# A recurrent layer's first operands ahead of its norm's root, and block-sum steps two and four in the twelve-tile down pairs

## The chip, the cores and the metric

The kernel runs on one core of a Trainium2 chip. The core has TensorE (matrix products, into PSUM), VectorE, ScalarE, GpSimd and SyncE, called PE, DVE, ACT, POOL and SP in the profile; PEld is TensorE's loading of the stationary operand. Each engine works through its own instructions in order and waits for others by semaphores. Weights come from device memory by DMA; the SP and POOL queues issue these transfers. The metric is device time of one execution in microseconds (us); lower is better.

## The reference, cut to what matters

The model is an encoder trunk of two residual layers over 256 tokens of 2048 features, in float32. Layer 0 mixes tokens by attention, layer 1 by a recurrent block; behind each mixer stands a gated feed-forward network of width 5632.

```python
for i in range(DEPTH):                       # DEPTH = 2
    h = rms_norm(x, norm_mix[i])             # x * rsqrt(mean(x*x) + EPS) * gain
    mix = attention_mixer(h, ...) if i % 2 == 0 else recurrent_mixer(h, ...)
    x = x + mix
    x = x + swiglu(rms_norm(x, norm_ffn[i]), ffn_w_gate[i], ffn_w_up[i], ffn_w_down[i])

def recurrent_mixer(h, w_in, conv_w, conv_b, w_a, b_a, w_i, b_i, lam, w_out):
    xb, yb = jnp.split(h @ w_in, 2, axis=-1)
    yb = gelu(yb)
    xb = depthwise_conv_centred(xb, conv_w, conv_b)      # width 4
    h_fwd, h_bwd = rg_lru(xb, ...), rg_lru(xb, ..., reverse=True)   # gates: block-diagonal products of xb
    return ((h_fwd + h_bwd) * yb) @ w_out

def swiglu(h, w_gate, w_up, w_down):
    return (silu(h @ w_gate) * (h @ w_up)) @ w_down
```

## The kernel before

**Products in three matmuls.** Every float32 operand is split into a rounded high part and the remainder as low part, and a product is three matmuls: high by high, high by low, low by high. Weights arrive in halves of 512 KB (eight 128x128 tiles). `load_half` loads one by the SP queue into `raw`, ScalarE rounds it to `hi` (L141) and VectorE subtracts to get `lo` (L142). Five buffers of each kind rotate, so these two engines can prepare halves ahead of TensorE.

**Pairs and block-sum steps.** In the feed-forward network `project_pair` works on two 512-wide columns of weights at once. A step `n` covers two 128-row tiles of the inner dimension. An ordinary step loads two halves, one for each column, and makes eight products (two columns, two token halves, two tiles), each 128x512. For steps listed in `forms` it makes seven products instead, by sums and differences of the blocks, as in fast matrix multiplication: `seven_forms` builds the weight sums, `x_forms` the operand sums. The weight sums start from one half loaded by SP, a second 256 KB load (`wx`), and a block `sr` that the POOL queue has fetched two such steps ahead, in two buffers, as a 512 KB copy and a 256 KB transfer that adds to it. ScalarE and VectorE then work at L319 to L328. Four of the seven products go to four extra PSUM banks (`p1, q5, q6, q7`, the tag `pm`) and `merge` (L401 to L405) adds these up once per pair, behind the last block-sum step; three go to the ordinary accumulators.

**The feed-forward network in parts.** The hidden width of 44 tiles is worked in `PARTS` of 12, 16 and 16 tiles. A part is three or four units (gate and up columns; each gives four hidden tiles) and then two down pairs, which multiply the part's hidden tiles back to 2048 columns and add to the residual `x_tok` (L581, L589). Units use block-sum steps `THREE = (1, 3, 5)`, the second, fourth and sixth step; so do down pairs of sixteen tiles. Down pairs of twelve tiles have six ordinary steps. `pair_plan` lets the first steps of a pair serve both columns and the last ones each column alone, so that the first column can be finished while the second goes on.

A unit's result is turned and split for the next product by work put into `owed` (a transpose at L860, sixteen copies at L866, the split at L873 and L874, and `x_forms` where a later step wants them). `settle` emits a few entries of it at a time, between steps of what follows.

**Who sets the order.** TensorE's order is that of the program text. On the other engines a planner places instructions by their readiness in its own timeline. `in_line` and `follow` pin some: casts and low parts keep their order among themselves, and `not_after(i, ahead)` makes the low part of the half `ahead` places on follow instruction `i`, which `settled` carries out.

**The norm of the recurrent layer.** `Norm.add(c)` is called as each of the four 512-wide columns of the residual is complete: sums of squares on ScalarE (L491), transposes on VectorE (L496), copies on both (L503), then four operand tiles with their gains (L478, L479). The root of the mean square is left out of the operands; it is multiplied in later. `finish` takes it (L520 to L530): a reduction, a logarithm and an exponential on ScalarE, one correction on VectorE, and a diagonal `ndg`. `stage`, emitted `NORM = 20` TensorE steps later, spreads the root over all partitions by matmuls with ones (L536) and ScalarE copies it to `nrb` (L538). For the last column, `first` calls `finish` right behind the squares, and the copies of that column must follow the root's last ScalarE instruction and the diagonal:

```python
fields["behind"] = self.finish() if last else [line.get(e) for e in ("act", "dve")]
...
behind = fields["behind"] if last else [line.get(e) for e in ("act", "dve")]
```

The first TensorE work of the recurrent layer is `project_two`: two columns of the input projection, 32 steps of three 128x256 matmuls (L409 to L411). The first 24 read only operand tiles of the first three columns; the last eight read the four tiles of the last column. It is a generator: `conv_branch` (the multiplication by the root, L905, and the convolution) for the first column is emitted before the last four steps of the second. The gates of the first block follow 24 steps into the next projections (`WHEN_FIRST`).

Of the kernel before, what the change touches and what calls it, by code (L numbers as in the profile page):

```python
# [12 lines left out]
F32 = mybir.dt.float32  # L13
F32R = mybir.dt.float32r
AF = mybir.ActivationFunctionType
ALU = mybir.AluOpType
AX = mybir.AxisListType

P = 128
# [9 lines left out]
THREE, TWO, SHORT = (1, 3, 5), (2, 5), 6  # L29
# [5 lines left out]
FOUR = WIDE // P  # L35
# [4 lines left out]
GRID_W = 64  # L40

WARM = 10
NORM = 20
FIRST = 6
KEY_SCALE = 20
KEY_TURN = (62, 68)
# [24 lines left out]
def trunk(ctx, tc, w, out):  # L71
    nc = tc.nc
    act, dve, pool, pe, sync = nc.scalar, nc.vector, nc.gpsimd, nc.tensor, nc.sync
# [13 lines left out]
    def nm(s):  # L87
        uid[0] += 1
        return f"{s}_{uid[0]}"
# [6 lines left out]
    newest = {}  # L96

    def follow(i, j):
        tc.add_manual_dep(
            i.ins, j.ins.name,  # L100
            mybir.DependencyInfo(mybir.DependencyClass.NoSync, mybir.DependencyReason.DATA),
            reason="order",
        )
        return i


    line = {}

    def in_line(eng, i):
        if eng in line:  # L110
            if line[eng] is not None:
                follow(i, line[eng])
            line[eng] = i
        return i

    due = {}

    def not_after(i, ahead=3):
        due.setdefault(taken[0] + ahead, []).append(i)

    def settled(i, n):
        for k in [k for k in due if k <= n]:
            for j in due.pop(k):
                follow(i, j)

    def load_half(src, n, pieces=1, then=None, before=None):
        raw = wp.tile([P, HALF, P], F32, tag="raw", name=nm("raw"), bufs=5)
        hi = wp.tile([P, HALF, P], F32R, tag="hi", name=nm("hi"), bufs=5)
        lo = wp.tile([P, HALF, P], F32R, tag="lo", name=nm("lo"), bufs=5)
        for i in range(pieces):  # L130
            sl = slice(i * n // pieces, (i + 1) * n // pieces)
            newest["load"] = sync.dma_start(out=raw[:, sl, :], in_=src[:, sl, :])
        newest["raw"] = raw
        if then:
            then()
        if before:
            before(raw)
        for i in range(pieces):
            sl = slice(i * n // pieces, (i + 1) * n // pieces)
            newest["tiles"] = hi, lo  # L140
            newest["cast"] = in_line("act", act.copy(hi[:, sl, :], raw[:, sl, :]))  # L141
            rest = in_line("dve", dve.tensor_tensor(lo[:, sl, :], raw[:, sl, :], hi[:, sl, :].bitcast(F32), ALU.subtract))  # L142
            settled(rest, taken[0] - 1)
        return [(hi[:, i, :], lo[:, i, :]) for i in range(n)]
# [24 lines left out]
    seven_at, ffn_ends = [], []  # L169

    def down_seven(n, alone):
        return () if alone else () if n == SHORT else THREE

    def ffn_order(l, base):
        units = [wide(f"w_gate{l}"), wide(f"w_up{l}")]
# [39 lines left out]
    taken = [0]  # L215
# [44 lines left out]
    def new_acc():  # L260
        return ps_a.tile([P, 2 * S], F32, tag="acc", name=nm("acc"))
# [35 lines left out]
    coming, ahead = [], []  # L297
# [120 lines left out]
    def project_sum(xs):  # L418
        bank = new_acc()
        for k0 in range(0, len(xs), HALF):  # L420
            sums(bank[:, :S], half(), xs, k0)
        return bank[:, :S], bank[:, S:]


    def project_two(xs, late):
        banks = [new_acc() for _ in range(2)]
        for t in banks:
            sums(t[:, :S], half(), xs, 0)
        rest = [half() for _ in range(2)]
        n = len(xs) - HALF - late  # L430
        for t, wt in zip(banks, rest):
            sums(t[:, :S], wt[:n], xs, HALF)
        for t, wt in zip(banks, rest):
            sums(t[:, :S], wt[n:], xs, HALF + n)
            yield t[:, :S], t[:, S:]
# [8 lines left out]
    ident = cst.tile([P, P], F32, tag="ident", name="ident")  # L444
# [20 lines left out]
    class Norm:  # L465
# [6 lines left out]
        def operand(self, x, wide=False):  # L472
            g = col(self.g[0], self.g[1] + len(self.xs))
            t = xp.tile([P, 2 * S], F32R, tag="xg", name=nm("xg"), bufs=16)
            hi, lo = (t[:, o : o + S] for o in (0, S))
            if wide:
                hi, lo = (v.rearrange("p (q t) -> p q t", t=32) for v in (hi, lo))
            i = act.activation(hi, x, AF.Copy, scale=g)  # L478
            dve.scalar_tensor_tensor(lo, x, g, hi.bitcast(F32), ALU.mult, ALU.subtract)  # L479
            self.xs.append(t)  # L480
            return i


        def add(self, c):
            last = c == NCOL - 1
            parts = []
            fields = {}

            def first():
                for a in range(2):  # L490
                    act.activation(tmp("nj", (P, WIDE), mybir.dt.bfloat16, 1), x_tok[:, a, c, :], AF.Square, accum_out=self.sums[:, a, c : c + 1])  # L491
                fields["behind"] = self.finish() if last else [line.get(e) for e in ("act", "dve")]
                fields["b"] = fp[0].tile([P, 2, FOUR, P], F32, tag="tb", name=nm("tb"))
                fields["f"] = fp[0].tile([P, 8, FOUR, 32], F32, tag="tf", name=nm("tf"))
                for a in range(2):
                    dve.transpose(fields["b"][:, a, :, :], x_tok[:, a, c, :])  # L496

            def copies(q):
                b, f = fields["b"], fields["f"]
                behind = fields["behind"] if last else [line.get(e) for e in ("act", "dve")]  # L500
                for i in range(4):
                    o, y = f[32 * i : 32 * i + 32, q::4, :, :], b[32 * q : 32 * q + 32, :, i, :]
                    n = (dve.tensor_copy if i % 2 else act.copy)(o, y.rearrange("p a (k t) -> p a k t", k=FOUR))  # L503
                    if behind and behind[i % 2] is not None:
                        follow(n, behind[i % 2])

            def operands():
                for k in range(FOUR):
                    self.operand(fields["f"][:, :, k, :], True)
                for n in THREE[1:] if self.seven else ():  # L510
                    if FOUR * c <= 2 * n < FOUR * c + FOUR:
                        self.forms[n] = x_forms(self.xs[2 * n], self.xs[2 * n + 1], f"nf{n}")

            owed.extend([first, *(partial(copies, q) for q in range(4)), operands])
            if last:
                settle(-1)

        def finish(self):
            ms = tmp("nrt", (P, 2))
            dve.tensor_reduce(ms, self.sums, AX.X, ALU.add)  # L520
            dve.tensor_scalar(ms, ms, 1.0 / D, EPS, ALU.mult, ALU.add)
            self.rt = rsqrt(ms, "nr")
            if not self.seven:
                return prev[0], self.spread()


        def spread(self):
            dg = tmp("ndg", bufs=1)
            for a in range(2):
                i = dve.tensor_scalar(dg[:, a * P : (a + 1) * P], ident, self.rt[:, a : a + 1], None, ALU.mult)  # L530

            def stage():
                pst = ps_m.tile([P, 2 * S], F32, tag="pm", name=nm("pm"))
                for a in range(2):
                    sl = slice(a * P, a * P + P)
                    pe.matmul(pst[:, sl], ones, dg[:, sl], start=True, stop=True)  # L536
                self.r = tmp("nrb", bufs=1)
                act.copy(self.r, pst[:, :S])  # L538

            later(NORM, stage)  # L540
            return i

# [54 lines left out]
    prev = [None]  # L599
# [293 lines left out]
    nr = Norm("norm_mix", KT)  # L893
# [106 lines left out]
    blk = nxt = None  # L1000
    for b in range(-1, NBLK):
        blk, nxt = nxt, Block(b + 1) if b + 1 < NBLK else None
        if blk:
            work = [partial(blk.gates, g) for g in range(4)]
            work += [partial(blk.decay, *u) for u in units]
            work += [partial(blk.scan, *u) for u in units]
            work += [blk.gelu] + [partial(blk.finish, j) for j in range(2)]
            when = WHEN_FIRST if not blk.b else WHEN if nxt else WHEN_LAST
            for t, fn in zip(when, work):
                later(t, fn)  # L1010
        if nxt:
            accs = (project_sum(nr.xs) for _ in range(2)) if blk else project_two(nr.xs, FOUR)
            nxt.xcs = [conv_branch(2 * b + 2 + i, t) for i, t in enumerate(accs)]
            if not blk:
                for g in range(GATE_BUFS):
                    load_gates(g)
        if blk:
            blk.ys = [gelu_branch(2 * b + i) for i in range(2)]
# [103 lines left out]
```

## Time and profile before

| | before |
|---|---|
| median of 3 runs | 1966.99 us (1964.8 to 1967.59) |
| profiled execution | 1964.75 us, span 1963.0 us |
| PE, PEld busy | 1954.5, 1660.3 us |
| DVE, ACT, POOL busy | 1686.6, 1344.2, 222.3 us |
| HBM traffic | 219 GB/s over the span |

Busy times are from the profile's page. Matmuls overlap in it and the ends of matmuls are modelled, so a busy TensorE says that instructions follow each other, not that each runs at its best. The lengths of VectorE and ScalarE instructions in time-ordered rows overlap their neighbours by some hundredths of a microsecond; the distance between starts is what one costs. Names like `xg` or `lo` are the program's tiles, L142 is line 142 of the kernel, and `x3` behind a row means three such instructions merged.

### The profile page before, as it was taken

How to read it: one execution, taken by the hardware profiler on the slowest of the kernel's cores; microseconds unless marked ns; L12 is line 12 of the kernel's file. 1: busy time of each engine (PE TensorE's matmuls, PEld its weight loads, DVE VectorE, ACT ScalarE, POOL GpSimd, SP SyncE). 2: the span in 40 equal slices, each digit the busy share in tenths (PEclk: the TensorE clock that was granted, in tenths of full speed). 3: DMA queues.
4: the chain of work that ended last, by engine and by line, in shares of the span. 5: the costliest groups of instructions: out<-in, count | busy, mean ns of one | idle time of the engine just before them, and what ended most of it. 6: DMA issues, size and time to landing. Idle time of an engine off the chain costs nothing.

```text
span 1963.0 us, 27585 instructions
## 1 busy us (share of the span) xinstructions
PE 1954.5 (100%) x9665; PEld 1660.3 (85%) x9665; DVE 1686.6 (86%) x2274; ACT 1344.2 (68%) x2051; POOL 222.3 (11%) x317
## 2 busy tenths in 40 slices
PE   9999999999999999999999999999999999999999
PEld 8888888888888888888899998888888888888887
DVE  6776989858999989999788986998768999989997
ACT  6666767655677556777799996767646776567763
POOL 0011000000011100101034331001001010011010
PEclk9999999999999999999999999999999999999999
DMA  8543667756677876776555546567757777677784
GB/s 340 186 140 140 209 207 243 237 202 225 207 247 243 267 247 215 232 233 232 193 176 174 195 160 219 194 205 239 250 189 226 239 239 256 232 242 236 233 261 164
DMA packets 134059, 430.75 MB, mean 219 GB/s; under 512 B 15008, under 2 KB 15904, under 8 KB 133664
## 3 DMA queue, kind: packets, MB, share of 16 engines
q1 hardware_dynamic: 109296, 362.11, 52.9%
q0 software_dynamic: 24480, 66.86, 13.2%
q8 instruction: 76, 1.25, 0.2%
q14 instruction: 63, 0.52, 0.1%
q10 hardware_dynamic: 144, 0.02, 0.0%
HBM read 426.83 MB, written 2.10 MB: 219 GB/s over the span
## 4 chain that ended last, share of the span: by engine, by line
PE 98%; ACT 1%; DVE 1%; issue 0%; DMA 0%; DVEq 0%; ACTq 0%
PE acc L356 63%; PE pm L356 12%; PE acc L272 10%; PE acc L410 3%; PE acc L409 3%; PE acc L411 3%; PE pm L272 1%; PE pm L410 1%; PE pm L409 1%; PE pm L411 1%; PE pm L743 1%; PE pm L775 1%; PE pm L761 0%; ACT sg L607 0%; ACT L607 0%
## 5 line engine op out<-in xcount | busy, mean ns | idle before, releaser
L142 DVE TENSOR_TENSOR lo<-raw,hi 128x1024 fp32r<-128x1024 f32 (+1 forms) x621 | 748.4, 1229 | 130.6 <-ACT hi L141 127.7
L141 ACT CAST hi<-raw 128x1024 fp32r<-128x1024 f32 (+1 forms) x621 | 638.0, 1046 | 310.4 <-PE acc L356 163.3
L356 PE MATMUL acc<-hi,xg 128*128 128x512 f32 x1920 | 612.7, 389 | 0.0
L356 PE MATMUL acc<-hi,act 128*128 128x512 f32 x1370 | 433.7, 390 | 0.2 <-DVE gl L920 0.2
L356 PEld LDWEIGHTS acc<-hi,xg 128*128 128x128 f32 x1920 | 360.4, 188 | 74.8
L356 PE MATMUL acc<-lo,xg 128*128 128x512 f32 x960 | 373.4, 389 | 0.0
L356 PEld LDWEIGHTS acc<-hi,act 128*128 128x128 f32 x1370 | 257.2, 188 | 53.6 <-DVE gl L920 0.7
L356 PE MATMUL acc<-lo,act 128*128 128x512 f32 x685 | 266.6, 389 | 0.0
L356 PEld LDWEIGHTS acc<-lo,xg 128*128 128x128 f32 x960 | 180.2, 188 | 37.4
L326 ACT CAST wxh<-raw 128x1024 fp32r<-128x1024 f32 x85 | 89.3, 1051 | 91.3 <-DVE raw L324 91.3
L356 PEld LDWEIGHTS acc<-lo,act 128*128 128x128 f32 x685 | 128.6, 188 | 26.0
L866 ACT COPY tf<-tb 32x256 f32<-32x256 f32 x352 | 142.1, 404 | 10.9 <-DVE tb L860 7.0
L409 PE MATMUL acc<-xg,hi 128*128 128x256 f32 x512 | 144.9, 283 | 1.1 <-ACT xg L478 1.1
L410 PE MATMUL acc<-xg,hi 128*128 128x256 f32 x512 | 144.8, 283 | 0.1
L411 PE MATMUL acc<-xg,lo 128*128 128x256 f32 x512 | 144.4, 282 | 0.0
L304 POOL DMA_DIRECT2D sr<-in_w_up_dram x64 | 35.6, 557 | 763.5 <-DVE lo L325 598.1
L321 ACT CAST hi<-sr 128x1024 fp32r<-128x1024 f32 x85 | 89.3, 1051 | 37.6 <-PE acc L356 27.1
L322 ACT CAST wxh<-wx 128x512 fp32r<-128x512 f32 x85 | 52.8, 621 | 90.1 <-DVE wx L319 55.0
L328 DVE TENSOR_TENSOR wxl<-raw,wxh 128x1024 fp32r<-128x1024 f32 x85 | 103.3, 1215 | 7.7 <-ACT wxh L326 7.5
L272 PE MATMUL acc<-hi,xg 128*128 128x512 f32 x320 | 107.6, 396 | 0.5 <-ACT hi L141 0.5
L325 DVE TENSOR_TENSOR lo<-sr,hi 128x1024 fp32r<-128x1024 f32 x85 | 103.6, 1218 | 0.0
L409 PEld LDWEIGHTS acc<-xg,hi 128*128 128x128 f32 x512 | 97.9, 191 | 1.3 <-ACT xg L478 1.3
(212 smaller groups left out, 3174.5 us busy)
## 6 DMA issues: line engine op xcount, KB each, us to landing
raw<-in_w_gate_dram SPq DMA_DIRECT2D x176, 512.0 KB, 5.3
raw<-in_w_down_dram SPq DMA_DIRECT2D x155, 512.0 KB, 5.1
raw<-in_w_up_dram SPq DMA_DIRECT2D x112, 512.0 KB, 5.4
sr<-in_w_up_dram POOLq DMA_DIRECT2D x64, 512.0 KB, 4.9
raw<-in_w_in_dram SPq DMA_DIRECT2D x64, 512.0 KB, 4.4
raw<-in_w_qkv_dram SPq DMA_DIRECT2D x46, 512.0 KB, 4.4
raw<-in_w_o_dram SPq DMA_DIRECT2D x32, 512.0 KB, 3.5
wx<-in_w_up_dram SPq DMA_DIRECT2D x64, 256.0 KB, 4.6
```

Source lines behind the costliest of these rows:

```text
L141: newest["cast"] = in_line("act", act.copy(hi[:, sl, :], raw[:, sl, :]))
L142: rest = in_line("dve", dve.tensor_tensor(lo[:, sl, :], raw[:, sl, :], hi[:, sl, :].bitcast(F32), ALU.subtract))
L272: pe.matmul(accs[a], x, wt[:, k, :], start=(k0 + k == 0 and n == 0), stop=(end and k == 1 and n == 2))
L321: in_line("act", act.copy(hi, raw))
L325: settled(in_line("dve", dve.tensor_tensor(lo, raw, hi[:].bitcast(F32), ALU.subtract)), taken[0] - 1)
L326: in_line("act", act.copy(xh[:, 1:, :], r1))
L328: in_line("dve", dve.tensor_tensor(xl[:, 1:, :], r1, xh[:, 1:, :].bitcast(F32), ALU.subtract))
L356: pe.matmul(acc, a, b, start=id(acc) not in begun, stop=last and i == 2)
L409: pe.matmul(o, hi, x[:, :S], start=start, stop=False)
L410: pe.matmul(o, hi, x[:, S:], start=False, stop=False)
L411: pe.matmul(o, lo, x[:, :S], start=False, stop=stop)
L866: n = act.copy(f[32 * i : 32 * i + 32, q::4, :, :], b[32 * q : 32 * q + 32, :, i, :, :])
```

## The change

Two edits in one. First, `down_seven` gives down pairs of twelve tiles the block-sum steps `THREE[:2]`, indices 1 and 3, the second and the fourth step. The plan of these pairs, four steps together and two for each column alone, stays. Each such pair then also runs `merge` and its adds to the residual behind the fourth step, the operand forms of these steps are made behind the first and second unit's result, and the POOL queue fetches their `sr` blocks.

Second, in the norm ahead of the recurrent layer (the one made without block sums) `finish` is called behind the last column's operands instead of behind its squares, and the copies of that column follow nothing. `not_after` gets an engine argument, and the ScalarE cast and the VectorE low part of the half four places on (the fifth of the new projection) must follow the last operand's two instructions. `NORM` goes from 20 to 31, so that `stage` stands ahead of the last of the 32 steps, and the two accumulators of `project_two` are taken as a list, so that both convolution branches are emitted behind it.

```diff
-NORM = 20
+NORM = 31
...
-    def not_after(i, ahead=3):
-        due.setdefault(taken[0] + ahead, []).append(i)
+    def not_after(i, ahead=3, eng="dve"):
+        due.setdefault((taken[0] + ahead, eng), []).append(i)
...
-    def settled(i, n):
-        for k in [k for k in due if k <= n]:
+    def settled(i, n, eng="dve"):
+        for k in [k for k in due if k[0] <= n and k[1] == eng]:
...
             newest["cast"] = in_line("act", act.copy(hi[:, sl, :], raw[:, sl, :]))
+            settled(newest["cast"], taken[0] - 1, "act")
...
     def down_seven(n, alone):
-        return () if alone else () if n == SHORT else THREE
+        return () if alone else THREE[:2] if n == SHORT else THREE
...
             i = act.activation(hi, x, AF.Copy, scale=g)
-            dve.scalar_tensor_tensor(lo, x, g, hi.bitcast(F32), ALU.mult, ALU.subtract)
+            newest["operand"] = i, dve.scalar_tensor_tensor(lo, x, g, hi.bitcast(F32), ALU.mult, ALU.subtract)
...
-                fields["behind"] = self.finish() if last else [line.get(e) for e in ("act", "dve")]
+                if last and self.seven:
+                    self.finish()
...
-                behind = fields["behind"] if last else [line.get(e) for e in ("act", "dve")]
+                behind = None if last else [line.get(e) for e in ("act", "dve")]
...
                     self.operand(fields["f"][:, :, k, :], True)
+                if last and not self.seven:
+                    for e, i in zip(("act", "dve"), newest["operand"]):
+                        not_after(i, 4, e)
+                    self.finish()
...
             if not self.seven:
-                return prev[0], self.spread()
+                self.spread()
...
-            accs = (project_sum(nr.xs) for _ in range(2)) if blk else project_two(nr.xs, FOUR)
+            accs = (project_sum(nr.xs) for _ in range(2)) if blk else list(project_two(nr.xs, FOUR))
```

More of the change, by code (lines that the diff above doesn't have):

```diff
@@ L540, in spread @@
             later(NORM, stage)
-            return i
     fp = []
```

2 lines of the change are left out of this document (1 added, 1 removed).

## The prediction

> **What bounds the kernel now.** I read the page's chain first, then TensorE's waits, then the chain in order of time, then windows and time-ordered rows at the places that the diff touches.
>
> ```profile
> PE 98%; ACT 1%; DVE 1%; issue 0%; DMA 0%; DVEq 0%; ACTq 0%
> ```
> ```profile
> PE pm L536 <- DVE ndg L530: 1.6, 1, 1.6
> PE acc L409 <- ACT xg L478: 1.1, 1, 1.1
> ```
> ```profile
> 373.26 82.28 PE acc L356 x363
> ```
>
> The first line is the chain that ended last, by engine; then the longest entries of TensorE's waits (total, times, longest); then a stretch of the chain (start, length, what, count). TensorE issues back to back almost everywhere, so the time falls by what is taken out of its stream and by its two real waits, which both stand at the start of the recurrent layer. The pitch of a 128x512 matmul is 82.28/363 = 0.2267 us. What remains is to see whether the engines that feed TensorE stay ahead of it.
>
> **Part 1: block-sum steps in the twelve-tile down pairs.** An ordinary step of a pair is 8 products of 3 matmuls, 24 x 0.2267 = 5.44 us; a block-sum step is 7 products, 4.76. Two layers, two pairs each, two steps each: 8 x 3 x 0.2267 = 5.44 us of TensorE removed, 2.72 per layer. That is the whole gain of this part.
>
> VectorE pays for it. Its rows in order of time (start, length, instruction):
>
> ```profile
> 366.53 0.69 DVE L319 TENSOR_TENSOR wx<-wx,raw 128x512 f32<-128x512 f32 x1
> ...
> 369.72 0.69 DVE L327 TENSOR_TENSOR wxl<-wx,wxh 128x512 fp32r<-128x512 f32 x1
> 370.32 1.22 DVE L328 TENSOR_TENSOR wxl<-raw,wxh 128x1024 fp32r<-128x1024 f32 x1
> 371.46 3.49 DVE L142 TENSOR_TENSOR lo<-raw,hi 128x1024 fp32r<-128x1024 f32 x3
> 374.87 0.68 DVE L402 TENSOR_TENSOR fg<-pm,fg 128x512 f32<-128x512 f32 x1
> ```
>
> The six operations of a block-sum step (L319 to L328) fill 366.53 to 371.46, 4.93 us; one L142 takes (374.87-371.46)/3 = 1.14. With the L142 of its own first half a step costs 6.07 in place of two L142, 2.28: +3.79, for the four of a layer +15.2. A 128x512 operation takes 0.60 back to back (369.72 to 370.32). Each pair gains four in the merge (L402 to L405) and four adds to the residual (L581): 16 x 0.60 = 9.6 per layer. The operand forms of steps two and four (x_forms, seven VectorE instructions, six of them on smaller tiles) are made once each: at most 7 x 0.60 = 4.2; I take half by the sizes, 4.2 for both. Together +29.0 us per layer. The windows that must hold it (start:end, length, then busy time of PE, PEld, DVE, ACT, POOL, granted clock, DMA share, GB/s) are the second and third unit with the pairs, the pairs alone, the unit after them, and three later units that carry such forms already:
>
> ```profile
> 302.60:449.94 147.34, 147.34 (x651) 122.00 (x650) 113.77 (x124) 92.53 (x127) 8.51 (x12) 1.00 0.67 222
> 384.66:449.94 65.28, 65.28 (x289) 54.05 (x288) 38.87 (x39) 32.93 (x42) 0.00 (x0) 1.00 0.57 199
> 449.94:491.50 41.56, 41.56 (x185) 34.42 (x184) 35.16 (x40) 22.97 (x25) 4.26 (x6) 1.00 0.74 240
> 491.50:616.00 124.50, 124.50 (x551) 103.10 (x550) 117.47 (x149) 90.15 (x129) 12.73 (x18) 1.00 0.74 239
> ```
>
> In the first, VectorE would have 113.8+29.0 = 142.8 us to do in 147.3-2.7 = 144.6 of TensorE: 99%. The last window runs gapless at 117.47/124.50 = 94.4%. Were that all that VectorE can sustain, it would need 142.8/0.944 = 151.3 and fall 6.7 us behind. What covers this is its lead:
>
> ```profile
> 420.22 1.05 ACT L141 CAST hi<-raw 128x1024 fp32r<-128x1024 f32 x1 [1.66 <-PE acc L356]
> 421.31 1.22 DVE L142 TENSOR_TENSOR lo<-raw,hi 128x1024 fp32r<-128x1024 f32 x1 [0.85 <-ACT hi L141]
> ```
>
> The cast at 420.22 begins as TensorE frees half 12 of the pairs (384.66 + 13 x 2.72 = 420.0, a half being 12 matmuls) and fills half 17, whose low part is done at 422.5 and wanted at 384.66 + 17 x 2.72 = 430.9: 8.4 us ahead. The next unit asks 35.16 of 41.56, so the lead is rebuilt before the second deficit. I cost it at nothing; without any lead it would be 6.7 per layer, and a gain is excluded, as work is only added. Nearer nothing, because 6.7 is below 8.4. ScalarE gets two more casts and, per pair, a merge copy: with 1.05 for the cast of a half, at most 4 x 2.1 + 2 x 1.05 = 10.5 on 32.93 in 62.6 us. SP issues a 256 KB load in place of a 512 KB one, POOL two transfers (512 and 256 KB): 0.5 MB more per step, 2 MB per layer, 33 GB/s on 199, no more than the neighbours' 240.
>
> One result comes due earlier: the last unit's four tiles, wanted by step five. The sixteen-tile pair has the same steps up to there, so its rows are the model (TensorE's first matmul of that pair; ScalarE's casts ahead of L873; VectorE's low part of the tiles):
>
> ```profile
> 615.86 0.39 PE L356 MATMUL acc<-hi,act 128*128 128x512 f32 x1
> ```
> ```profile
> 632.38 2.00 ACT L141 CAST hi<-raw 128x1024 fp32r<-128x1024 f32 x2
> ```
> ```profile
> 635.92 1.22 DVE L874 TENSOR_TENSOR act<-tf,act 128x1024 fp32r<-128x1024 f32 x1
> ```
>
> With block sums in steps two and four step five begins 2 x 5.44 + 2 x 4.76 = 20.4 after the pair's start, and its first matmul with a low part at 20.85. L874 ends at 637.14, 21.28 after. That is 0.43 late, 0.9 for two layers. Bounds: nothing, if L873 is planned ahead of the two casts (2.0); 0.43+2.0 = 2.4 per layer, if two more casts go ahead of it. I take the row's own case. Part 1: -5.44+0.9 = -4.5.
>
> [...]
>
> **Part 2: operands ahead of the root.** TensorE, VectorE and ScalarE at the start of the recurrent layer:
>
> ```profile
> 949.74 0.28 PE L409 MATMUL acc<-xg,hi 128*128 128x256 f32 x1
> ...
> 956.57 0.28 PE L409 MATMUL acc<-xg,hi 128*128 128x256 f32 x1
> ...
> 958.72 0.71 PE L536 MATMUL pm<-ndg,ones 128*128 128x128 f32 x4 [1.62 <-DVE ndg L530]
> 959.18 0.36 PE L409 MATMUL acc<-xg,hi 128*128 128x256 f32 x1
> ...
> 965.07 0.28 PE L409 MATMUL acc<-xg,hi 128*128 128x256 f32 x1
> ```
> ```profile
> 951.68 0.71 DVE L496 STREAM_TRANSPOSE tb<-x_tok 128x512 f32<-128x512 f32 x1
> ...
> 953.41 0.15 DVE L520 TENSOR_REDUCE nrt<-nsq 128x2 f32<-128x8 f32 x1
> ...
> 958.89 2.38 DVE L503 COPY tf<-tb 32x256 f32<-32x256 f32 x8
> ...
> 964.19 0.43 DVE L905 TENSOR_TENSOR cb<-acc,nrb 128x256 f32<-128x256 f32 x1 [0.60 <-PE acc L411]
> ```
> ```profile
> 956.63 3.29 ACT L503 COPY tf<-tb 32x256 f32<-32x256 f32 x8
> ...
> 961.36 1.71 ACT L478 ACTIVATE xg<-tf,pk 128x256 fp32r<-128x256 f32 x4 [1.05 <-DVE tf L503]
> ```
>
> A step of the projection is three 128x256 matmuls, one of each of L409 to L411. Twenty steps stand ahead of the stage at L536, and 949.74 to 956.57 is nineteen pitches: 0.36 each. All 32 steps and the stage (958.72 to 959.18, 0.46) need 11.98; TensorE takes 15.33 to the next block at 965.07. So 3.35 us is lost there, and that is the ceiling of this part.
>
> The transposed tile is there at 952.4, but its copies were ordered behind the root: ScalarE's run at 956.63, VectorE's at 958.89. Freed, ScalarE copies until 955.7 and makes the four operands until 957.4, the first at 956.1, its low part about 0.5 later. The last eight steps, which read them, begin at 949.74 + 24 x 0.36 = 958.4. That wait goes. The cast and low part of the fifth half from there are now pinned behind the operands (to 957.9); that half is wanted at 961.7 and cast and low part take 1.05+1.22, so the pin costs nothing. The SP queue's loads, which wait for low parts to free their buffers, are for halves four or more further on.
>
> The root is late next. It issues on VectorE and ScalarE alone, and from L520 to the diagonal took 953.41 to 958.89, 5.5 us, with casts and low parts of about 1 us between its short instructions. Now eight copies and four operands stand ahead of it on each engine. VectorE's copies end at 952.4+2.4 = 954.8, and it then has nothing until ScalarE's first operand at 956.1; if the planner puts L520 there, the diagonal is ready at 960.3. The stage, now 31 steps in, wants it at 949.74 + 31 x 0.36 = 960.9: no wait. If L520 starts only behind the operands, 957.9+5.5 = 963.4, 2.5 us are lost, with the last step and all later blocks queued behind the stage on TensorE. I take no wait.
>
> Then the first gates come 3.35 sooner, while the convolution branch, which waits for the stage (until 960.9+0.7) and its copy to SBUF (a 128x256 operation, by L478's row 0.4), starts at 962.0 in place of 964.19: 2.2 sooner, so up to 1.15 of new wait in front of the gates. POOL's two small memsets per branch wait with it and hold nothing. Taking both accumulators as a list costs no more, as the second ends within the stage's time. I take half, 0.6, since fewer low parts are left to run between the branch's operations. Part 2: -3.35+0.6 = -2.7; bounds -3.35 and +0.3 (2.5+1.15 lost).
>
> **The sum.** -4.5-2.7 = -7.2 us. The profiled execution took 1964.75 (span 1963.0), 2.24 under the median of 1966.99: 1957.5 in such an execution, 1959.8 as a median.
>
> **The rivals.**
> - Root in the way still, so that the reordering does not do what it says: the diagonal at 963.4 eats part 2, and 1966.99-4.5 = 1962.5. For it: the order on VectorE and ScalarE is the planner's, and the old chain was mostly queueing. Against: VectorE's empty microsecond.
> - Last unit late: three more casts ahead of L873, 0.43+3.0 = 3.4 per layer: 1966.99-5.44+6.8-2.7 = 1965.7, no measurable change. Against: the model row has two in all.
> - Slower, VectorE becoming the bound. Place: second unit to the pairs' end; price 6.7 per layer if the lead is spent on arrival: 1966.99-5.44+13.4-2.7 = 1972.3. It decides from (5.44+2.7)/2 = 4.1 lost per layer. For it: 99%. Against: 8.4 us of lead, and the light unit behind.
> - Late POOL sums, from POOL's rows and the DMA issues:
>
> ```profile
> 370.11 0.55 POOL L304 DMA_DIRECT2D sr<-in_w_up_dram  x1 [7.96 <-DVE lo L325]
> 375.25 0.85 POOL L305 DMA_DIRECT2D sr<-in_w_up_dram  x1 [4.59 <-DMA sr<-in_w_up_dram]
> ```
> ```profile
> sr<-in_w_down_dram POOLq DMA_DIRECT2D x21, 256.0 KB, 7.4
> ```
>
> The two transfers of a step take 5.1+7.4 = 12.5. Those issued at 370.11 will serve step four of the first pair, at 384.66 + 2 x 5.44 + 4.76 = 400.3, 30 us on; less 8.4 for conversion, 9 us are spare. At twice the time 3.4 is lost per step, 27 in all: 1987. [...]
>
> **How the numbers follow.** Both parts as summed 0.55; root in the way 0.21; last unit late 0.12; VectorE the bound 0.10; late sums 0.02. Differences under 0.2% (3.9 us) cannot be told from no change here. The first two are faster, 0.76; the third the same, 0.12; the last two slower, 0.12. The range goes down to both ceilings, 1966.99-5.44-3.35 = 1958.2, less the 2.2 by which an execution can lie under the median: 1956.0; and up to the last-unit case: 1965.7.
>
> **What would show it.** Block-sum products in the twelve-tile pairs, which then last 62.6 us in place of 65.3, with VectorE above 90% there and at most a short TensorE wait on L874; no wait on L478; the stage 31 steps in, without a wait; a small one on L439 ahead of the gates. I am wrong if TensorE waits on L142, L327 or L328 after the second unit, if L536 still waits, or if waits appear elsewhere because the planner ordered VectorE and ScalarE anew.

## The result and the profile after

The changed kernel took 1962.31 us in the median of 12 executions (1959.47 to 1964.66), the kernel before 1966.19 (1964.8 to 1967.59, 12 executions beside it). The ratio is 0.998 with a 95% interval of 0.9972 to 0.9989: 3.9 us less. The profiled executions hide this: 1964.66 us after (span 1962.8, mean granted clock 0.998) against 1964.75 before (span 1963.0, clock 1.000). So the two traces can only be compared place by place.

The chain that ended last by engine, and all of TensorE's waits from 0.5 us up (total, times, longest), of the kernel after:

```profile
PE 96%; ACT 2%; DVE 1%; issue 1%; DMA 0%; DVEq 0%; ACTq 0%
```
```profile
PE pm L459 <- POOL ones L456: 1.0, 1, 1.0
PE pm L410 <- DVE xs L439: 0.9, 1, 0.9
PE pm L411 <- DVE xs L440: 0.7, 1, 0.7
PE acc L357 <- DVE act L879: 0.5, 2, 0.3
```

TensorE is still the chain. The two waits of before, on `ndg` and on `xg`, are gone. In their place stand two on `xs`, the operand that the first gates read (the split at L439 and L440), and two of about 0.25 on the last unit's low part (L879, which was L874). The first line was there before.

Three stretches of the chain in order of time (start, length, what, count), before and then after: the kernel's first long stretch, the one that begins late in the first layer, and one behind the recurrent layer.

```profile
50.39 18.36 PE acc L272 x81
...
894.82 55.08 PE acc L356 x243
...
1187.96 39.73 PE acc L356 x174
```
```profile
52.02 18.36 PE acc L273 x81
...
895.06 55.08 PE acc L357 x243
...
1189.98 39.73 PE acc L357 x174
```

Between the second and third row, where the recurrent layer lies, before takes 293.14 us and after 294.92: in this execution the reordered norm cost 1.78 instead of gaining. The first rows say that after was already 1.63 late when nothing of the change had run. That is no effect of the change: another execution of the same kernel, quoted below, has that row at 50.18. The rest lies in the feed-forward layers: each of the two stretches with the twelve-tile pairs is 2.17 shorter, and a stretch of later units (from about 770 to 895) is, in this execution only, 0.78 longer. 1.63-2 x 2.17+0.78+1.78 = -0.15, and the spans differ by -0.2.

**The pairs.** Windows (start:end, length, then busy time of PE, PEld, DVE, ACT, POOL, granted clock, DMA share, GB/s) of the two twelve-tile pairs, and of the second and third unit with them, after:

```profile
386.29:449.39 63.10, 62.85 (x277) 51.74 (x276) 59.47 (x72) 38.44 (x51) 5.67 (x8) 1.00 0.72 232
304.23:449.39 145.16, 144.91 (x639) 119.70 (x638) 137.87 (x171) 98.91 (x138) 14.16 (x20) 1.00 0.74 236
```

The pairs last 63.10 us, from their first matmul to the first of the next unit (65.28 before). VectorE is busy for 59.47 of them (94%), and for 137.87 of 145.16 in the longer window (95%); TensorE has no gap there but 0.25. That gap, on VectorE and TensorE in order of time:

```profile
406.29 1.22 DVE L879 TENSOR_TENSOR act<-tf,act 128x1024 fp32r<-128x1024 f32 x1
```
```profile
407.56 0.73 PE L357 MATMUL acc<-hi,act 128*128 128x512 f32 x2 [0.25 <-DVE act L879]
```

The 0.25 counts from the modelled end of the matmul ahead. That matmul starts at 406.92, so this one comes 0.64 behind it in place of 0.23, and the pairs are 0.54 longer than the 65.28-2.72 = 62.56 that the removed products would leave.

**The recurrent layer's start.** TensorE's projection, the stage and the first gates; then VectorE; then one-microsecond windows over the gates:

```profile
949.97 0.28 PE L410 MATMUL acc<-xg,hi 128*128 128x256 f32 x1
...
961.13 0.61 PE L542 MATMUL pm<-ndg,ones 128*128 128x128 f32 x4
...
961.93 0.28 PE L410 MATMUL acc<-xg,hi 128*128 128x256 f32 x1
...
970.82 0.35 PE L410 MATMUL pm<-xs,ghi 128*128 128x256 f32 x1
971.82 0.39 PE L411 MATMUL pm<-xs,ghi 128*128 128x256 f32 x1 [0.65 <-DVE xs L440]
...
973.25 0.58 PE L410 MATMUL pm<-xs,ghi 128*128 128x256 f32 x1 [0.93 <-DVE xs L439]
...
975.85 0.41 PE L410 MATMUL acc<-xg,hi 128*128 128x256 f32 x1
...
979.69 0.37 PE L410 MATMUL pm<-xs,ghi 128*128 128x256 f32 x1
```
```profile
958.85 1.23 DVE L143 TENSOR_TENSOR lo<-raw,hi 128x1024 fp32r<-128x1024 f32 x1
959.99 0.48 DVE L536 TENSOR_SCALAR ndg<-ident,nr 128x128 f32<-128x128 f32 x2
960.38 3.49 DVE L143 TENSOR_TENSOR lo<-raw,hi 128x1024 fp32r<-128x1024 f32 x3
963.79 0.74 DVE L910 TENSOR_TENSOR cb<-acc,nrb 128x256 f32<-128x256 f32 x2
...
973.50 0.41 DVE L440 TENSOR_TENSOR xs<-xc,xs 128x256 fp32r<-128x256 f32 x1
```
```profile
971.00:972.00 1.00, 0.35 (x2) 0.18 (x2) 1.00 (x4) 1.00 (x2) 0.13 (x2) 1.00 0.96 389
972.00:973.00 1.00, 0.32 (x2) 0.12 (x2) 1.00 (x2) 0.21 (x1) 0.00 (x0) 1.00 0.90 328
973.00:974.00 1.00, 0.61 (x2) 0.32 (x2) 1.00 (x4) 0.00 (x0) 0.00 (x0) 0.53 0.37 143
974.00:975.00 1.00, 1.00 (x5) 1.00 (x6) 0.86 (x3) 0.00 (x0) 0.00 (x0) 0.50 0.72 217
...
979.00:980.00 1.00, 1.00 (x7) 1.00 (x6) 0.00 (x0) 0.77 (x2) 0.00 (x0) 0.56 0.64 178
```

The projection takes 961.93-949.97 = 11.96 us (15.33 before), and the stage comes without a wait. But the two convolution branches, from the multiplication at 963.79 to the end of the second split at 973.91, run through the time at which the gates are wanted. TensorE reaches these at 970.82 and is past them only at 975.85: 5.03 us, where before took 1.66 (974.06 to 975.72, four gate steps of 0.36 to 0.58). And with 0.53 and 0.56 in the clock column, TensorE ran at half its clock from 973.06 to 979.88 (a share of 0.06 of the one slice and 0.12 of the other at full clock): 6.8 us.

### The profile page after: what moved, and what is told of

Same layout as the page of the kernel before. It is cut to its first block, busy times and chain, and to the rows that moved or that the text cites. A ratio compares the mean times of both kernels' runs of the same rounds, so it can differ in the third digit from the quotient of the medians.

```text
span 1962.8 us, 27715 instructions
## 1 busy us (share of the span) xinstructions
PE 1955.2 (100%) x9641; PEld 1659.9 (85%) x9641; DVE 1737.4 (89%) x2374; ACT 1357.9 (69%) x2075; POOL 233.7 (12%) x333
## 4 chain that ended last, share of the span: by engine, by line
PE 96%; ACT 2%; DVE 1%; issue 1%; DMA 0%; DVEq 0%; ACTq 0%
PE acc L357 60%; PE pm L357 12%; PE acc L273 10%; PE acc L410 3%; PE acc L411 3%; PE acc L412 3%; PE pm L273 1%; PE pm L411 1%; PE pm L412 1%; PE pm L410 1%; ACT tf L871 1%; DVE lo L143 1%; PE pm L748 1%; PE pm L780 1%; PE pm L766 0%
## 5 line engine op out<-in xcount | busy, mean ns | idle before, releaser
L143 DVE TENSOR_TENSOR lo<-raw,hi 128x1024 fp32r<-128x1024 f32 (+1 forms) x613 | 736.7, 1227 | 87.8 <-ACT hi L141 81.9
L141 ACT CAST hi<-raw 128x1024 fp32r<-128x1024 f32 (+1 forms) x613 | 627.4, 1046 | 255.3 <-PE acc L357 93.0
L357 PE MATMUL acc<-hi,act 128*128 128x512 f32 x1258 | 402.1, 390 | 0.8 <-DVE act L879 0.5
L357 PEld LDWEIGHTS acc<-hi,act 128*128 128x128 f32 x1258 | 236.0, 188 | 50.6 <-DVE act L879 1.4
L357 PE MATMUL acc<-lo,act 128*128 128x512 f32 x629 | 244.8, 389 | 0.0
L327 ACT CAST wxh<-raw 128x1024 fp32r<-128x1024 f32 x93 | 97.8, 1052 | 110.8 <-DVE raw L325 110.8
L357 PEld LDWEIGHTS acc<-lo,act 128*128 128x128 f32 x629 | 118.2, 188 | 23.8
L322 ACT CAST hi<-sr 128x1024 fp32r<-128x1024 f32 x93 | 97.7, 1051 | 39.2 <-PE acc L357 28.4
L329 DVE TENSOR_TENSOR wxl<-raw,wxh 128x1024 fp32r<-128x1024 f32 x93 | 112.7, 1211 | 6.9 <-ACT wxh L327 6.9
L326 DVE TENSOR_TENSOR lo<-sr,hi 128x1024 fp32r<-128x1024 f32 x93 | 113.1, 1216 | 0.0
```

Source lines behind the costliest of these rows:

```text
L322: in_line("act", act.copy(hi, raw))
L326: settled(in_line("dve", dve.tensor_tensor(lo, raw, hi[:].bitcast(F32), ALU.subtract)), taken[0] - 1)
L327: in_line("act", act.copy(xh[:, 1:, :], r1))
L329: in_line("dve", dve.tensor_tensor(xl[:, 1:, :], r1, xh[:, 1:, :].bitcast(F32), ALU.subtract))
L357: pe.matmul(acc, a, b, start=id(acc) not in begun, stop=last and i == 2)
```

## The experiments

The theory with which the runs were made: part 1 gives what was summed for it. Part 2 takes 3.4 us out of the projection and gives it back at the first gates, because the convolution branches end hardly sooner than before; and the halved clock behind that idle time costs some more. The rivals: the block sums cost something elsewhere that the norm's gain covers; the branches are late not because of what is ordered ahead of them but because they are long; the low clock has nothing to do with the gates.

### Each part alone

The kernel before with part 1 only:

```diff
-        return () if alone else () if n == SHORT else THREE
+        return () if alone else THREE[:2] if n == SHORT else THREE
```

> Only the block-sum steps of the twelve-tile pairs; the norm as before. My theory: 5.44 us of TensorE out, 0.55 per layer given back at L874 (L879 in the changed kernel), so 4.3 us under the kernel before; the two waits at the start of the recurrent layer as before (1.6 and 1.1 us); granted clock as in the kernel before. Rival, the denser stream lowers the clock: mean clocks of 0.998 to 0.999 here too and 2 us or less gained.

Measured: 1961.13 us (1960.09 to 1962.96) beside 1965.44, ratio 0.9978 (0.9969 to 0.9987): -4.3. The waits on `ndg` and `xg` stand as before, the one on the low part is 0.5 in all, the clock 1.000 in all ten executions.

The kernel after without part 1:

```diff
-        return () if alone else THREE[:2] if n == SHORT else THREE
+        return () if alone else () if n == SHORT else THREE
```

> Only the reordered norm; the twelve-tile pairs as before. My theory: 3.4 us gained ahead of the first gates and 1.6 us lost in a wait on the convolution branch at the gates (L439, L440), after which the granted clock is 0.5 for some 6.7 us in part of the executions, 3.3 us more: between 1.7 us under and 1.6 us over the kernel before, with mean clocks from 0.998 to 1.000. Rival, the reordering only moves the loss and no clock is involved: 1.7 us under in every execution, clock 1.000.

Measured: 1965.46 us (1963.71 to 1966.62) beside 1965.44, ratio 0.9999 (0.999 to 1.0007). Part 2 gains nothing in the median, and the parts add up within their intervals: -4.3 and 0.0 against -3.9 for both. Its executions fall in two groups by their mean granted clock: 1.000 in six, with a mean of 1964.84 us, and 0.999 in five, with 1966.15. At full clock part 2 gains 0.9 against the mean of before (1965.71, clock 1.000), at the other it loses 0.4.

### The same kernel once more

The kernel after, unchanged, on another chip than the two runs above.

> The changed kernel once more, beside the others on one chip: 1962 us, clocks of 0.998 to 1.000, and the slower executions of it at the lower clocks. If the clock has no part in its time, times and clocks are unrelated.

Measured: 1961.51 us (1959.38 to 1963.21) beside 1965.33, ratio 0.9979 (0.997 to 0.9988). The profiled execution was one of full clock, 1959.38 us. One row of its chain, and its projection and gates in order of time:

```profile
50.18 18.36 PE acc L273 x81
```
```profile
947.40 0.28 PE L410 MATMUL acc<-xg,hi 128*128 128x256 f32 x1
...
968.24 0.36 PE L410 MATMUL pm<-xs,ghi 128*128 128x256 f32 x1
969.25 0.38 PE L411 MATMUL pm<-xs,ghi 128*128 128x256 f32 x1 [0.65 <-DVE xs L440]
...
970.68 0.39 PE L410 MATMUL pm<-xs,ghi 128*128 128x256 f32 x1 [0.92 <-DVE xs L439]
...
972.45 0.28 PE L410 MATMUL acc<-xg,hi 128*128 128x256 f32 x1
...
974.59 0.28 PE L410 MATMUL pm<-xs,ghi 128*128 128x256 f32 x1
```
The waits are the same to 0.01 us, and the mean clock of this execution is 1.000. The gates take 972.45-968.24 = 4.21 us in place of 5.03, and the six steps behind them 2.14 in place of 979.69-975.85 = 3.84. The halved clock, where it lasts 6.8 us, thus costs 0.82+1.70 = 2.5 us. From the projection's start to the end of the gates this execution takes 25.05, before 975.72-949.74 = 25.98: 0.9 gained, as in the run above.

Over both sets of the kernel after, 23 executions: clock 1.000 in 8, mean 1960.1 us; 0.999 in 12, 1962.3; 0.998 in 3, 1963.6. Two executions in three pay; spread over all of them that is (12 x 2.2 + 3 x 3.5)/23 = 1.6 us. These differences between the groups also hold whatever else varies from one execution to the next.

### Moving the gates

Later, so that the branches are done in time:

```diff
-WHEN_FIRST = (24, 30, 36, 42) + WHEN[4:]
+WHEN_FIRST = (34, 40, 46, 52) + WHEN[4:]
```

> The changed kernel with the first block's four gate products 10 steps (3.6 us) later in TensorE's stream, WHEN_FIRST 34, 40, 46, 52. My theory: no wait on L439 or L440, no stretch at clock 0.5, all mean clocks near 1.000, 5.44-1.1+3.4 = 7.7 us under the kernel before and 3 to 4 us under the changed kernel's median. Rival, the lowered clock belongs to the denser stream: clocks stay at 0.998 to 0.999 and only 1.6 us is gained on the changed kernel. Another rival: the wait comes back at the decays, which now follow the gates closely: 1 to 2 us of waits there and no more gain than 5 us in all.

Measured: 1962.24 us (1961.42 to 1965.23) beside 1965.44, ratio 0.9986 (0.9977 to 0.9995): -3.2, no better. TensorE's waits have lost both lines on `xs` at the gates, but have a new first line:

```profile
PE acc L410 <- DVE act L440: 2.6, 1, 2.6
```

It stands at 1007 us, where the next accumulators are free only when the first block's chain of vector work, now later, has ended; the granted clock is 0.86 between 1000 and 1010 and 0.83 between 1010 and 1012, which at half clock makes an estimated 2 x (1.4+0.34) = 3.5 us. So the idle time moves rather than going away, and the clock falls there too. Here the mean clock does not part the executions (1962.79 us at 0.999, 1963.01 at 1.000), so what its fall costs in this version stays open.

Earlier, so that TensorE idles more:

```diff
-WHEN_FIRST = (24, 30, 36, 42) + WHEN[4:]
+WHEN_FIRST = (18, 24, 30, 36) + WHEN[4:]
```

> The changed kernel with the first block's gates 6 steps (2.2 us) earlier, WHEN_FIRST 18, 24, 30, 36, so that the suspected wait is doubled. My theory: 3.8 us of waits on L439 and L440, the clock halved in nearly every execution: 2 to 5 us slower than the changed kernel, mean clocks 0.998. Rival, the clock has nothing to do with the wait: 2.2 us slower, clocks spread as in the changed kernel.

Measured: 1962.67 us (1961.89 to 1965.3), ratio 0.9986 (0.9977 to 0.9995): -2.8. The first of TensorE's waits, and the two windows in which the clock falls and comes back (it is 0.50 between them):

```profile
PE pm L410 <- issue: 2.9, 1, 2.9
```
```profile
970.00:971.00 1.00, 0.79 (x3) 0.69 (x3) 1.00 (x4) 0.10 (x1) 0.07 (x2) 0.63 0.98 303
...
973.00:974.00 1.00, 1.00 (x8) 1.00 (x7) 0.00 (x0) 0.94 (x2) 0.26 (x1) 0.66 0.00 0
```

The profile names no releaser for this wait; the first branch's cast (L439) ends at 969.11, and the gate starts at 969.21. A second wait, on the split, is 0.65.

Waiting 3.5 us in place of 1.6 to 1.9 costs only 1.1 us more against its own before, which the intervals do not tell from nothing. The branches end hardly sooner (23.35 us after the projection's start in place of 23.94), and what TensorE does not do ahead of the gates it does behind them. The clock was below 1.000 in each of the 11 executions. In the profiled one (0.999) the half clock lasted 3.4 us, from 970.26 to 973.68 by the two shares, and not 6.8.

The kernel before with early gates, to see whether idle time there lowers the clock without the change:

```diff
-WHEN_FIRST = (24, 30, 36, 42) + WHEN[4:]
+WHEN_FIRST = (14, 20, 26, 32) + WHEN[4:]
```

> The kernel before with nothing but the first block's gates 10 steps (3.6 us) earlier, WHEN_FIRST 14, 20, 26, 32, so that TensorE waits at the gates some 3.6 us on the same convolution branches. My theory, that an idle stretch there lowers the clock whatever the rest of the kernel is: waits on L439 and L440 of 3 to 4 us, stretches at clock 0.5 behind them, mean clocks 0.998 to 0.999 and up to 3.3 us more: 2 to 6 us slower than the kernel before. If only the order of work counts, the later projection steps fill in behind the gates, the clock stays at 1.000 and the time is within 1 us of the kernel before. If the lowered clock belongs to the block sums or to the reordered norm: clock 1.000, whatever the time.

Measured: 1967.03 us (1966.55 to 1969.31) beside 1965.33, ratio 1.0009 (1.0001 to 1.0018), clock 1.000 in all 11. This run missed its aim. The planner took the branches sooner too, and only this much was idle at the gates:

```profile
PE pm L409 <- issue: 0.8, 1, 0.8
PE pm L410 <- DVE xs L439: 0.3, 1, 0.3
```

It shows that 1.1 us of idle time there left the clock at 1.000; it does not show that a longer one without the change would lower it.

### What stands ahead of the branches

The kernel after without the two pins, so that the fifth half's cast and low part need not follow the operands:

```diff
                 if last and not self.seven:
-                    for e, i in zip(("act", "dve"), newest["operand"]):
-                        not_after(i, 4, e)
                     self.finish()
```

> The changed kernel without its two pins of the fifth half behind the last operand. The prediction costed the pins at nothing. If that holds: same waits and the same time as the changed kernel within 1 us. Rival, the pins are what puts three low parts in front of the convolution branch: without them the branch starts up to 2 us sooner, the wait at the gates is shorter by as much and the clock stays up; then 1 to 3 us faster than the changed kernel. Third: without them the operands come late and TensorE waits on L479 again, 1 us or more.

Measured: 1958.45 us (1957.75 to 1959.66) beside 1965.45, ratio 0.9964 (0.9952 to 0.9977), clock 1.000 throughout: -7.0, which is 3.1 better than with the pins. One of its waits, VectorE's branches, TensorE's first gate:

```profile
PE acc L411 <- DVE xg L480: 0.9, 1, 0.9
```
```profile
961.88 0.75 DVE L908 TENSOR_TENSOR cb<-acc,nrb 128x256 f32<-128x256 f32 x2
...
969.51 0.42 DVE L440 TENSOR_TENSOR xs<-xc,xs 128x256 fp32r<-128x256 f32 x1
```
```profile
970.08 0.28 PE L410 MATMUL pm<-xs,ghi 128*128 128x256 f32 x1
```

The projection starts at 948.05 here. The gates are wanted 22.03 us later (20.85 with the pins), because the operands come 0.9 late and the root with them; but the second split ends at 969.93, 21.88 after the start, in place of 23.94, and no gate waits. At full clock the pins save 1.2 in the projection and lose 2.8 at the gates (here 971.51-970.08 = 1.43 in place of 4.21). With the 1.6 that the clock costs on average, 3.2 is lost in all, against 3.1 measured.

The opposite remedy, the pins kept and the branches put ahead of the low parts: the low part of the half three places on must follow the second split.

```diff
-        dve.tensor_tensor(dst[:, S:], src, dst[:, :S].bitcast(F32), ALU.subtract)
+        newest["split"] = dve.tensor_tensor(dst[:, S:], src, dst[:, :S].bitcast(F32), ALU.subtract)
...
             if not blk:
+                not_after(newest["split"], 3)
```

> The changed kernel, with one pin more: the low part of the half three places on must follow the last instruction of the two first convolution branches, so that VectorE runs the branches before three low parts and not between them. My theory: the branches' way through VectorE's queue, 963.8 to 973.9 in the changed kernel, is what the gates wait for. They should end near 969, the waits on L439 and L440 (1.6 us) and the stretch at clock 0.5 go, mean clocks 1.000, and the time is 5.4-1.1+3.4 = 7.7 us under the kernel before, about 3.5 under the changed kernel's median. Rival, the branches are late because of the root and its copy (962.1): the wait at the gates stays near 1.6 us. Other rival: the low parts that now come later make TensorE wait on L143 for 1 to 2 us, and half of the gain is lost there.

Measured: 1957.21 us (1956.32 to 1957.41) beside 1965.45, ratio 0.9957 (0.9944 to 0.9969), clock 1.000 throughout: -8.2, 4.4 better than the change. VectorE, and TensorE's first gate:

```profile
960.06 0.75 DVE L910 TENSOR_TENSOR cb<-acc,nrb 128x256 f32<-128x256 f32 x2
...
964.04 0.75 DVE L440 TENSOR_TENSOR xs<-xc,xs 128x256 fp32r<-128x256 f32 x2
```
```profile
967.97 0.28 PE L410 MATMUL pm<-xs,ghi 128*128 128x256 f32 x1
```

The two branches take 964.79-960.06 = 4.7 us in place of 10.1, and are done 3.2 us before the gates. So they are not long; low parts of other halves made them so. No other wait appeared.

Both remedies of small waits together, the run above with the last unit's split put ahead of the next half's cast and low part:

```diff
-                act.copy(hi, f)
-                dve.tensor_tensor(lo, f, hi.bitcast(F32), ALU.subtract)
+                i = act.copy(hi, f)
+                j = dve.tensor_tensor(lo, f, hi.bitcast(F32), ALU.subtract)
                 hid.extend(h[:, k, :] for k in range(FOUR))
+                if len(hid) == PARTS[0] == parts:
+                    not_after(i, 0, "act")
+                    not_after(j, 0)
```

> As the run with the branches first, and in the twelve-tile pairs the split of the last unit's tiles (L878, L879) pinned ahead of the next half's cast and low part. My theory: L879 then ends some 2 us sooner, its two waits of TensorE go, and 1.1 us more is gained: 8.8 us under the kernel before. Rival: VectorE is short there and the wait moves to the low part of the half that now follows (L143), no gain on the other run.

Measured: 1955.51 us (1955.1 to 1956.41) beside 1965.45, ratio 0.995 (0.9936 to 0.9964): -9.9 (the interval is -12.6 to -7.1), and 1.7 better than the run above. This version beats both kernels. Nothing is left of TensorE's waits from 0.2 us up but these:

```profile
PE pm L459 <- POOL ones L456: 1.0, 1, 1.0
PE acc L357 <- DVE gl L928: 0.2, 1, 0.2
```

Last, that version without the change's own two pins, the same two lines taken out as above.

> The run with both added pins, but without the change's own two pins behind the last operand. My theory: these pins only keep TensorE from a wait of 0.9 us on the operands (L480); with the branches pinned they no longer cost anything, so without them it is about 0.9 us slower than with both, 1956.4 us. Rival: they cost in any case; then faster than 1955.5.

Measured: 1957.67 us (1956.69 to 1957.72) beside 1965.33, ratio 0.9959 (0.9946 to 0.9971): -7.7, 2.3 worse than with them.

```profile
PE acc L357 <- DVE gl L926: 1.2, 1, 1.2
...
PE acc L411 <- DVE xg L480: 0.9, 1, 0.9
```

The gates come 968.88-946.86 = 22.02 us behind the projection's start in place of 967.67-947.08 = 20.59, and a wait on `gl`, further down the same layer, has grown from 0.2 to 1.2: 2.4 together. With the branches placed, the operand pins pay; without, they cost.

One measure leaves out the start of the kernel and the feed-forward layers: the stretch between the second and third row of the chain shown first, in one profiled execution of each version.

| version | us |
|---|---|
| before; block sums only | 293.14; 293.13 |
| norm only; after at full clock | 292.22; 292.23 |
| after with the half clock | 294.92 |
| after without the operand pins | 290.62 |
| branches first; with the last unit's split first too | 289.19; 289.19 |
| the last one without the operand pins | 291.62 |

## Why the prediction was right and wrong

The sum of -7.2 us was forecast, a median of 1959.8; -3.9 came, 1962.31, within the range and on the forecast side. One term was right and one mis-sized. That the whole still fell within the range was in part luck. Part 2, 0.0 measured alone, lies within its own bounds of -3.35 and +0.3, but the upper one was made of a wait on the root, which did not come, and of 1.15 at the gates, where 2.6 and the clock came.

**Part 1 was right**: -4.5 forecast, -4.3 measured alone. The pairs last 63.10 us, 0.54 more than the 62.6 of the products alone. This is the last unit's low part, the wait that the row of the sixteen-tile pair had announced: it ends 21.22 us after the pairs' start (forecast 21.28) and costs 1.1 for both layers in place of 0.9. The run that put it first also took this wait away. The rival of "last unit late" at 3.4 per layer did not come.

**VectorE did not become the bound.** The 99% were 95%, 137.87 us against 142.8: the added work was 137.87-113.77 = 24.1 us in that window and not 29.0. Which of the summed operations were too high was not separated; half of the operand forms and the sixteen merge and residual adds were estimates. The lead held in every window of the twelve-tile pairs. It was short elsewhere in the profiled execution: in later units, which already had block sums before, TensorE's weight loads waited 0.50 us for L326 at 809 and 0.25 at 851, and 0.28 and 0.19 for L329 (L328 before, one of the signs named for being wrong) at 790 and 801. The second execution of the same kernel has no such wait between 780 and 815, nor has before anywhere. **Late POOL sums** did not come either; the row of the DMA issues after is

```profile
sr<-in_w_down_dram POOLq DMA_DIRECT2D x29, 256.0 KB, 7.4
```

with the same 7.4 us to landing as before, while VectorE is 94% busy in the pairs. The 512 KB copies from `in_w_down_dram` land in 4.8 us in both kernels, POOL's two kinds from `in_w_up_dram` in 4.9 and 7.1: no median of its transfers became longer.

**The projection was right.** The ceiling of 3.35 was realised to 3.37. The diagonal was forecast for 960.3 and was ready at 960.47, in an execution whose projection began 0.23 later; the stage found it there. "Root in the way" fell: neither the kernel after nor the version with part 2 alone has a wait at the stage.

**Two steps of part 2 failed.** The first is "so the pin costs nothing". It looked only at whether the fifth half would be late on TensorE, and it is not. But the pin holds back a queue. Without it two low parts run ahead of the operands (at 954.32 and 956.37 in the run without pins) and one stands between the diagonal and the branches; with it none runs ahead, one stands before the diagonal (958.85) and three behind it (960.38 to 963.79). The branches, forecast to start at 962.0, start at 963.79, and more low parts run between their operations. Taking the pins away changes the time by -3.1, giving the branches the place ahead of the low parts by -4.4.

The second is "I take half, 0.6". The gap between the gates' gain (3.5 us sooner against the projection's start, 24.32 to 20.85) and the branches' (the second split 24.86 after that start before, 974.60 at L439, and 23.94 now) is 2.6 us, and that is what the gates take longer at full clock: 4.21-1.66 = 2.55. So the clean worth of part 2 is -3.4+2.6 = -0.8, as its executions at full clock show (-0.9) and the stretch of the recurrent layer (292.23-293.14 = -0.9). The bound of 1.15 for this wait assumed that the branches start when their inputs are there.

**What the prediction did not hold at all** is the fall of TensorE's clock behind these waits, to 0.50 for 6.8 us in the profiled execution. The remaining difference, from -0.9 to 0.0 in the median of part 2 alone, goes with it by its groups of executions; the interval of that run by itself (-2.0 to +1.4) is wider than this difference.

## What to carry to other kernels

An instruction that is held back takes its whole queue with it: where order is kept among casts or among low parts, a pin must be costed by what then stands behind the pinned place, on that engine, up to the next result that TensorE wants, not by the deadline of the pinned instruction alone (the two pins cost 3.1 us here). A stall removed ahead of a dependent chain is only worth what the chain itself moves (here 0.8 of 3.4 us), so ask first which engine's order sets that chain's end; here a pin on the chain's far end was worth as much again as the change (-4.4 beside -3.9). And where a change trades its waits for shorter ones close together (here 1.6 and 1.1 us for 0.65 and 0.93, with a clock of 0.50 behind them), look at the clock column of the execution, and at the clocks of many executions, before the sum is called done.

## What the runs showed of the hardware

**Behind short waits at the gates the clock fell.** Before has waits of 1.6 and 1.1 us at the root and the operands, some 2 us apart, and a mean clock of 1.000 in 61 of the 62 executions beside the experiments. (The other has 0.949 and 1966.48 us, within the times of the rest; nothing here explains it.) After has 0.65 and 0.93 (and 0.34 where the clock is full) with two matmuls between them, and the clock fell to 0.50 for 6.8 us in the profiled execution; the mean clock is under 1.000 in 15 of its 23. With waits of 2.9 and 0.7 it is so in 11 of 11; in the five versions whose gates stand in their place and have no listed wait (block sums only, no pins, branches first, both remedies, both without the operand pins) in none of 30. In the two slices ahead of the drop TensorE was busy for 0.35 and 0.32. The cost is not in proportion to the idle time: 2.5 us for waits of under 2. Nor does idle time alone decide it, for before idles longer and keeps its clock, and so does the second execution of the kernel after, with the same waits.

**The half clock came in two lengths**: 6.82 us in the profiled execution of the kernel after (mean clock 0.998), and 3.42 in the version with earlier gates, an estimated 3.5 in that with later ones (0.999 each). One stretch of 3.42 in a span of 1960 lowers the mean to an estimated 1-0.5 x 3.42/1960 = 0.9991, one of 6.82 to 0.9983. By this estimate most of the slower executions, those at 0.999, had the short one, and the 2.5 us are the price of the long one.

**What brings the fall is not settled.** A mean under 1.000 comes in 15 of 23 executions of one kernel, no wait at its gates was above 0.93 us in the two that were profiled, and the longest wait ahead of a drop in any profile was 2.9. Whether the length of a wait or the share of busy time around it counts, these runs do not show; the run meant to bring a wait of some 3.6 us into the kernel before did not bring it.

**The start of the kernel varies by itself**: the same row of the same program at 52.02 in one execution and at 50.18 in another, which is nearly half of what the change was worth. The first stretch of matmuls in the chain, of the kernel after and of its second execution:

```profile
5.91 5.29 PE acc L273 x12
```
```profile
6.38 2.79 PE acc L273 x11
```

In the first, a matmul takes 5.29/12 = 0.44 us (the six from 7.23 to 9.79 come every 0.43), in the second 2.79/11 = 0.25. So the one began at little more than half the other's pace, while its clock column reads 1.00 in each window of 2 us from 0 to 12: the granted clock does not show this difference. What decides it wasn't tried.
